# A transposed block by VectorE, both 32-blocks of a head in one product, and the decays of four heads in one product

## The chip, the cores and the metric

The kernel runs on one core of one Trainium2 chip. The metric is the device time of one execution in microseconds. The core has a matrix engine (TensorE, in the profile PE, its weight loads PEld), a vector engine (DVE), a scalar engine (ACT), GpSimd (POOL), and SyncE (SP), which issues most DMAs. Each engine works through a queue of its own in order, and semaphores tie the queues together.

## The reference

An encoder trunk with one hybrid layer (DEPTH is 1) over 2064 positions (16 meta tokens and 2048 inputs) with 1024 channels: layer norm, a combined input projection, a Fourier mixer and a gated DeltaNet side by side, gates, an output projection, and an MLP. The change touches the DeltaNet alone, which has 4 heads of 128 channels and runs in both directions. Cut to what matters:

```python
def chunked_gated_delta_rule(q, k, v, beta, g):
    g_cum = jnp.cumsum(g, axis=-1)
    diff = g_cum[..., :, None] - g_cum[..., None, :]
    decay_incl = jnp.exp(jnp.where(lower_incl, diff, -jnp.inf))
    decay_strict = jnp.where(lower_strict, decay_incl, 0.0)
    l_mat = jnp.einsum("rbhncd,rbhnsd->rbhncs", k_beta, k) * decay_strict
    unit_lower = l_mat + jnp.eye(CHUNK, dtype=l_mat.dtype)
    rhs = jnp.concatenate([v_beta, k_beta * jnp.exp(g_cum)[..., None]], axis=-1)
    sol = lax.linalg.triangular_solve(unit_lower, rhs, left_side=True, lower=True, unit_diagonal=True)
    ...
    def step(S, inp):
        val, kcd, qd, at, kt, cd = inp
        v_new = val - jnp.einsum("rbhcd,rbhde->rbhce", kcd, S)
        o = jnp.einsum("rbhcd,rbhde->rbhce", qd, S) + jnp.einsum("rbhcs,rbhse->rbhce", at, v_new)
        S = S * cd[..., None, None] + jnp.einsum("rbhcd,rbhce->rbhde", kt, v_new)
        return S, o
```

So for each chunk, head and direction a matrix of decays is needed, and the inverse of a unit triangular matrix; the chunks are then scanned one after the other.

## The kernel before

The kernel uses chunks of 128 positions: 16 chunks, and a short one of 16 positions for the meta tokens. Matrix products of the projections and of the MLP take f16 operands in three partial products (`mm3`, L95 to L97) and are arranged as Strassen products. The DeltaNet's own products are in f32; the trace shows each of them as two instructions on TensorE.

The work around the change lies in two stages.

**The preparation** (from about 520 to 840 us). `phase_zg` runs the projections of the gates on TensorE, group after group, and calls `next(side)` between them; `side` is the generator `Delta.prep`. It calls `stage2` for every chunk. `stage2` first calls `decay` for each direction, 32 times in all, and once more for the meta chunk (`meta`).

- `decay` forms, for one chunk and direction, E = exp(sums of g between two positions) for four heads at once. For each head it multiplies a 0/1 triangle by the head's column of g on VectorE (L1064, tile `gT`). On TensorE a product of a bf16 identity with a table of 0 and -1e30 (L1067) starts the PSUM bank `psg`, and four products, one for each head, with `gT` as weights and another triangle as the moving operand, add the sums of g (L1070). ScalarE takes exp (L1073).
- Then `stage2` forms the products of keys and queries (L1092), scales them with E on VectorE (L1097 for N, L1100 for A), takes the 32x32 diagonal blocks out (`diag`), and writes N and A to DRAM.
- `invert_blocks` inverts the diagonal blocks on VectorE (L997, L999).
- At the end of `prep`, `solve` runs for step 0 in both directions, with its PSUM from the pool `psg`.

PSUM tiles `psg` come from a pool of 3.

**The scan** (`phase_delta`, 995 to 1243 us). For step s it runs `step(s, d)` for both directions d, and between their parts `solve(s + 1, d)`, with its PSUM tiles from the pool `psh`. The function `go` and the list of its calls write out by hand in which order the parts follow. The instructions of a queue are then ordered when the program is built, and the trace shows small departures from the source order.

- `step` has five f32 products of 128x128 per head: with the state (L1264 and L1272), with the inverse (L1281), into the state (L1289) and into the output (L1301). Between them stand VectorE (L1266, L1295, L1307 or L1309) and ScalarE (L1275, L1284).
- `solve` builds the inverse X of the 128x128 triangular matrix, and its transpose XT, from the four inverted 32x32 diagonal blocks (L1171 and L1172 put them in place). In a first round it joins each pair of 32-blocks to a 64-block, in a second round the two 64-blocks. The first round is: product N by XT for each of the two pairs of a head (L1178), minus the result to V on ScalarE (L1181), product V by X (L1185), a further product X by V that gives one off-diagonal block transposed (L1187), a copy of that one to XT on ScalarE (L1188), and copies to X on VectorE (L1190). The second round is L1194, L1195, L1199 and L1200.

In `solve`, `blk(b)` is the b-th range of 32, `pair(a, z)` the z-th block of pair a, and f, s are 0, 1 in the forward direction and 1, 0 in the backward one. `cols(t, h, z)` takes, for head h, the z-th 32 columns of both pairs, 64 columns in all.

Of the kernel before, what the change touches and what calls it, by code (L numbers as in the profile page):

```python
# [12 lines left out]
AF = mybir.ActivationFunctionType  # L13
ALU = mybir.AluOpType
# [12 lines left out]
HD = 4  # L27
# [980 lines left out]
class Delta:  # L1008
# [48 lines left out]
    def decay(self, n, d, r):  # L1057

        k, nc, sp = self.k, self.k.nc, self.sp
        gs = k.g[:r, n, 4 * d:4 * d + 4]  # L1060
        gT = sp.tile([P, HD, P], F32, name="gT", bufs=2)
        m = (k.tls, k.tus)[d][:r, :r]
        for h in range(HD):
            nc.vector.tensor_scalar(gT[:r, h, :r], m, gs[:, h:h + 1], None, op0=ALU.mult)  # L1064
        yield
        ps = self.pg.tile([P, HD, P], F32, name="psg")
        nc.tensor.matmul(ps[:r, :, :r], lhsT=self.idb[:r, :r],  # L1067
                         rhs=self.mneg[:r, d, :r].unsqueeze(1).broadcast_to([r, HD, r]), start=True, stop=False)
        for h in range(HD):
            nc.tensor.matmul(ps[:r, h, :r], lhsT=gT[:r, h, :r], rhs=(k.tui, k.tli)[d][:r, :r],  # L1070
                             start=False, stop=h == HD - 1)
        E = sp.tile([P, HD, P], F32, name="E", bufs=2)
        nc.scalar.activation(out=E[:r, :, :r], in_=ps[:r, :, :r], func=AF.Exp)  # L1073
        return E
# [82 lines left out]
    def solve(self, step, d, sp, pp, pname):  # L1157

        k, nc = self.k, self.k.nc
        N = self.N[step, d]  # L1160
        ad = sp.tile([P, HD, 32], F32, name="ad", bufs=2)
        o = ((step % 4) * 2 + d) * 16
        (nc.scalar if step == 1 else nc.sync).dma_start(out=ad, in_=self.d2[step // 4][o:o + 16].rearrange("(h b) r j -> (b r) h j", b=4))
        X, XT, V, W = self.X[d][step % 2], self.XT[d], self.V[d], self.W[d]
        blk = lambda b: slice(32 * b, 32 * b + 32)
        half = lambda a: slice(64 * a, 64 * a + 64)
        f, s = ((0, 1), (1, 0))[d]
        pair = lambda a, z: blk(2 * a + z)
        x, xt = (XT, X) if d == 0 else (X, XT)
        for b in range(4):  # L1170
            nc.vector.transpose(xt[blk(b), :, blk(b)], ad[blk(b)])  # L1171
            nc.scalar.copy(x[blk(b), :, blk(b)], ad[blk(b)])  # L1172
        yield
        cols = lambda t, h, z: t[:, h].rearrange("p (a z c) -> p a z c", z=2, c=32)[:, :, z]
        ps = pp.tile([P, HD, P], F32, name=pname)
        for h in range(HD):
            for a in range(2):
                nc.tensor.matmul(ps[:32, h, blk(a)], lhsT=N[:, h, pair(a, s)], rhs=XT[:, h, pair(a, f)],  # L1178
                                 start=True, stop=True)
        for a in range(2):  # L1180
            nc.scalar.activation(out=V[pair(a, s), :, blk(a)], in_=ps[:32, :, blk(a)], func=AF.Copy, scale=-1.0)  # L1181
        yield
        ps = pp.tile([P, HD, P], F32, name=pname)
        for h in range(HD):
            nc.tensor.matmul(ps[:64, h, :64], lhsT=V[:, h], rhs=cols(X, h, s), start=True, stop=True)  # L1185
        for h in range(HD):
            nc.tensor.matmul(ps[:32, h, 64:96], lhsT=X[:, h, pair(f, s)], rhs=V[:, h, blk(f)], start=True, stop=True)  # L1187
        nc.scalar.copy(XT[pair(f, s), :, pair(f, f)], ps[:32, :, 64:96])  # L1188
        for a in range(2):
            nc.vector.tensor_copy(X[pair(a, f), :, pair(a, s)], ps[blk(a), :, blk(a)])  # L1190
        yield
        ps = pp.tile([P, HD, P], F32, name=pname)
        for h in range(HD):
            nc.tensor.matmul(ps[:64, h, :64], lhsT=N[:, h, half(s)], rhs=XT[:, h, half(f)], start=True, stop=True)  # L1194
        nc.scalar.activation(out=W[half(s)], in_=ps[:64, :, :64], func=AF.Copy, scale=-1.0)  # L1195
        yield
        ps = pp.tile([P, HD, P], F32, name=pname)
        for h in range(HD):
            nc.tensor.matmul(ps[:64, h, :64], lhsT=W[:, h], rhs=X[:, h, half(s)], start=True, stop=True)  # L1199
        nc.vector.tensor_copy(X[half(f), :, half(s)], ps[:64, :, :64])  # L1200
# [734 lines left out]
```

## Time and profile before

| | |
|---|---|
| median of 3 runs | 2729.1 us (2728.21 to 2729.52) |
| the profiled execution | 2723.02 us |
| span of its profile | 2721.2 us |
| mean granted TensorE clock | 0.988 |
| solves (32), products of L1178 | 8 each, 16 instructions |
| decays | 32 of 128 positions, one of 16 |

The profile is of one execution. A row of a timeline has the start in us, the length in us, the engine, the line of the kernel, the operation, output and inputs, the shapes, and how many instructions follow each other; in square brackets stands the idle time before it and what ended that. `128*32 128x32` means that 128 rows by 32 columns of weights are in the array, and 128x32 is the moving operand. Lengths of instructions that follow each other overlap, on TensorE above all: what one costs is read from start to start. A row of a group has the count, then the busy time in us, the mean length of one in ns, and the idle time of the engine just before them with what ended most of it. A row of waits has the engine and line that waited, what it waited for, the total in us, how often, and the longest.

### The profile page before, as it was taken

How to read it: one execution, taken by the hardware profiler on the slowest of the kernel's cores; microseconds unless marked ns; L12 is line 12 of the kernel's file. 1: busy time of each engine (PE TensorE's matmuls, PEld its weight loads, DVE VectorE, ACT ScalarE, POOL GpSimd, SP SyncE). 2: the span in 40 equal slices, each digit the busy share in tenths (PEclk: the TensorE clock that was granted, in tenths of full speed). 3: DMA queues.
4: the chain of work that ended last, by engine and by line, in shares of the span. 5: the costliest groups of instructions: out<-in, count | busy, mean ns of one | idle time of the engine just before them, and what ended most of it. 6: DMA issues, size and time to landing. Idle time of an engine off the chain costs nothing.

```text
span 2721.2 us, 42002 instructions
## 1 busy us (share of the span) xinstructions
PE 2604.6 (96%) x15087; PEld 1394.3 (51%) x15087; DVE 1950.3 (72%) x3793; ACT 1212.5 (45%) x2784; POOL 402.0 (15%) x559
## 2 busy tenths in 40 slices
PE   7988999999899989999999999999999999999997
PEld 6455545555454459995444444444444444444443
DVE  7589887888877326687867688888888645554556
ACT  5444665655553335674222544444454432222232
POOL 1000231310100001362256400000001200000003
PEclk9999999999999999999999999999999999999999
DMA  7468476699888758766722874444447633333311
GB/s 262 157 209 301 167 252 170 198 289 304 280 307 304 245 187 250 232 204 195 233 87 84 237 255 152 148 142 144 155 171 269 225 105 102 104 101 101 101 42 74
DMA packets 321219, 513.39 MB, mean 189 GB/s; under 512 B 83697, under 2 KB 135873, under 8 KB 317041
## 3 DMA queue, kind: packets, MB, share of 16 engines
q1 hardware_dynamic: 317088, 506.30, 56.5%
q10 hardware_dynamic: 3920, 4.40, 0.5%
q8 instruction: 118, 1.93, 0.3%
q14 instruction: 93, 0.75, 0.1%
HBM read 307.10 MB, written 203.50 MB: 188 GB/s over the span
## 4 chain that ended last, share of the span: by engine, by line
PE 67%; DVE 12%; DMA 6%; POOL 4%; ACT 3%; issue 3%; SPq 1%; DVEq 0%; POOLq 0%; ACTq 0%
PE mm L95 17%; PE mm L97 17%; PE mm L96 17%; DVE wu L59 1%; PE psc L1264 1%; PE psc L1289 1%; PE psc L1281 1%; PE psc L1301 1%; DVE hid L529 1%; PE psc L1272 1%; PE psf L95 1%; PE psm L95 1%; POOL hr L1412 1%; PE psm L97 1%; PE psm L96 1%
## 5 line engine op out<-in xcount | busy, mean ns | idle before, releaser
L95 PE MATMUL mm<-hb,wu 128*128 128x512 f16 x1280 | 487.1, 381 | 5.0 <-ACT ex L485 2.3
L97 PE MATMUL mm<-hb,wu 128*128 128x512 f16 x1280 | 487.3, 381 | 0.0
L96 PE MATMUL mm<-hb,wu 128*128 128x512 f16 x1280 | 487.2, 381 | 0.0
L1626 DVE TENSOR_TENSOR acc<-acc,mm 128x512 f32<-128x512 f32 x420 | 285.7, 684 | 147.9 <-PE mm L97 147.2
L95 PE MATMUL mm<-wdn,hid 128*128 128x512 f16 x904 | 342.1, 379 | 13.4 <-DVE acc L1626 13.3
L96 PE MATMUL mm<-wdn,hid 128*128 128x512 f16 x904 | 342.4, 379 | 0.0
L97 PE MATMUL mm<-wdn,hid 128*128 128x512 f16 x904 | 342.2, 379 | 0.2 <-DVE hid L529 0.2
L96 PEld LDWEIGHTS <-wu 128*128 128x128 f16 x1912 | 185.8, 98 | 218.7 <-issue 16.9
L97 PEld LDWEIGHTS <-wu 128*128 128x128 f16 x1912 | 185.6, 98 | 216.9 <-issue 7.4
L95 PEld LDWEIGHTS <-wu 128*128 128x128 f16 x1912 | 186.0, 98 | 210.3 <-issue 5.1
L95 PE MATMUL mm<-ht,wu 128*128 128x512 f16 x512 | 194.6, 380 | 5.5 <-DVE c L652 3.4
L529 DVE TENSOR_TENSOR hid<-c,hid 128x512 f16<-128x512 f32 x158 | 107.7, 688 | 124.8 <-ACT hid L528 124.6
L96 PE MATMUL mm<-ht,wu 128*128 128x512 f16 x512 | 194.5, 380 | 0.0
L97 PE MATMUL mm<-ht,wu 128*128 128x512 f16 x512 | 194.3, 380 | 0.0
L66 POOL TENSOR_SCALAR ln_rs<-ln_mv 128x1 f32<-128x1 f32 (+1 forms) x49 | 14.0, 285 | 1171.0 <-DVE ln_mv L76 1160.9
L528 ACT CAST hid<-c 128x512 f16<-128x512 f32 x158 | 95.7, 614 | 183.8 <-PE mm L97 155.2
L96 PEld LDWEIGHTS <-hid 128*128 128x128 f16 x904 | 88.4, 98 | 122.7 <-issue 19.8
L800 DVE SCALAR_TENSOR_TENSOR conv<-rawc,cw,conv 128x512 f32<-128x512 f32 x192 | 134.8, 744 | 15.4 <-ACT conv L798 14.9
L58 ACT ACTIVATE wdn<-raw 128x512 f16<-128x512 f32 x78 | 46.4, 622 | 222.7 <-PE mm L97 187.3
L97 PEld LDWEIGHTS <-hid 128*128 128x128 f16 x904 | 88.3, 98 | 108.1 <-DVE hid L529 2.2
L95 PEld LDWEIGHTS <-hid 128*128 128x128 f16 x904 | 88.4, 98 | 107.2 <-ACT hid L528 1.2
L58 ACT ACTIVATE wu<-raw 128x512 f16<-128x512 f32 x145 | 88.0, 622 | 74.4 <-PE mm L97 37.2
(388 smaller groups left out, 4999.5 us busy)
## 6 DMA issues: line engine op xcount, KB each, us to landing
wu<-op SPq DMA_DIRECT2D x245, 256.0 KB
op<-wu SPq DMA_DIRECT2D x203, 256.0 KB
wdn<-op SPq DMA_DIRECT2D x112, 256.0 KB
op<-wdn SPq DMA_DIRECT2D x98, 256.0 KB
kq<-kqd SPq DMA_DIRECT2D x46, 512.0 KB
raw<-in_w_down SPq DMA_DIRECT2D x36, 512.0 KB
raw<-in_w_qz SPq DMA_DIRECT2D x32, 512.0 KB
gt<-c SPq DMA_DIRECT2D x64, 256.0 KB
```

The costliest lines, as they stand in the source:

```text
L58: nc.scalar.activation(out=hi, in_=src, func=AF.Copy, scale=scale)
L59: nc.vector.scalar_tensor_tensor(out=lo, in0=src, scalar=scale, in1=hi, op0=ALU.mult, op1=ALU.subtract)
L95: mm(ps, lhsT=whi(q), rhs=xhi(q), start=first and q == 0, stop=False, skip_group_check=skip)
L96: mm(ps, lhsT=whi(q), rhs=xlo(q), start=False, stop=False, skip_group_check=skip)
L97: mm(ps, lhsT=wlo(q), rhs=xhi(q), start=False, stop=last and q == nk - 1, skip_group_check=skip)
L528: k.nc.scalar.copy(t[:, 0], src)
L529: k.nc.vector.tensor_tensor(out=t[:, 1], in0=src, in1=t[:, 0], op=ALU.subtract)
L800: nc.vector.scalar_tensor_tensor(out=s, in0=src[:, j:j + m], scalar=cw[:, c, j:j + 1], in1=s, op0=ALU.mult, op1=ALU.add)
L1264: nc.tensor.matmul(ps[:, h], lhsT=kq[:, h, 0], rhs=S[:, h], start=True, stop=True)
L1272: nc.tensor.matmul(psq[:, h], lhsT=kq[:, h, 1], rhs=S[:, h], start=True, stop=True)
L1281: nc.tensor.matmul(psv[:, h], lhsT=T_[:, h], rhs=R[:, h], start=True, stop=True)
L1626: nc.vector.tensor_tensor(out=c, in0=c, in1=ps, op=ALU.add)
```

## The change

In `decay` the four TENSOR_SCALAR of VectorE become one TENSOR_TENSOR over four heads, with both operands broadcast: the triangle over the heads, g over the columns. The two triangles trade places, so that the weights are the same for all heads and `gT` is the moving operand; the four products become one with 512 moving columns. The sums are the same ones.

In `solve` the two products of a head at L1178 become one: its weights are all 128 columns of N, its moving operand the 64 columns of XT that both products used. The two wanted 32x32 blocks then lie at other partitions of the PSUM tile, and L1181 reads them there. The product at L1187 is left out. The block that it gave is taken from the result of L1185, by a transpose of 32x32 blocks on VectorE, ahead of the two copies at L1190; ScalarE's copy (L1188) goes.

```diff
         gT = sp.tile([P, HD, P], F32, name="gT", bufs=2)
-        m = (k.tls, k.tus)[d][:r, :r]
-        for h in range(HD):
-            nc.vector.tensor_scalar(gT[:r, h, :r], m, gs[:, h:h + 1], None, op0=ALU.mult)
+        m = (k.tui, k.tli)[d][:r, :r]
+        nc.vector.tensor_tensor(out=gT[:r, :, :r], in0=m.unsqueeze(1).broadcast_to([r, HD, r]),
+                                in1=gs.unsqueeze(2).broadcast_to([r, HD, r]), op=ALU.mult)
         yield
...
-        for h in range(HD):
-            nc.tensor.matmul(ps[:r, h, :r], lhsT=gT[:r, h, :r], rhs=(k.tui, k.tli)[d][:r, :r],
-                             start=False, stop=h == HD - 1)
+        nc.tensor.matmul(ps[:r, :, :r], lhsT=(k.tls, k.tus)[d][:r, :r], rhs=gT[:r, :, :r], start=False, stop=True)
...
         for h in range(HD):
-            for a in range(2):
-                nc.tensor.matmul(ps[:32, h, blk(a)], lhsT=N[:, h, pair(a, s)], rhs=XT[:, h, pair(a, f)],
-                                 start=True, stop=True)
+            nc.tensor.matmul(ps[:, h, :64], lhsT=N[:, h], rhs=cols(XT, h, f), start=True, stop=True)
         for a in range(2):
-            nc.scalar.activation(out=V[pair(a, s), :, blk(a)], in_=ps[:32, :, blk(a)], func=AF.Copy, scale=-1.0)
+            nc.scalar.activation(out=V[pair(a, s), :, blk(a)], in_=ps[pair(a, s), :, blk(a)], func=AF.Copy, scale=-1.0)
         yield
...
-        for h in range(HD):
-            nc.tensor.matmul(ps[:32, h, 64:96], lhsT=X[:, h, pair(f, s)], rhs=V[:, h, blk(f)], start=True, stop=True)
-        nc.scalar.copy(XT[pair(f, s), :, pair(f, f)], ps[:32, :, 64:96])
+        nc.vector.transpose(XT[pair(f, s), :, pair(f, f)], ps[blk(f), :, blk(f)])
         for a in range(2):
             nc.vector.tensor_copy(X[pair(a, f), :, pair(a, s)], ps[blk(a), :, blk(a)])
```

## The prediction

> **What bounds the kernel now.** I read the page first, then the busy times by stage, then TensorE's order of instructions inside one step.
>
> ```profile
> span 2721.2 us, 42002 instructions
> PE 2604.6 (96%) x15087; PEld 1394.3 (51%) x15087; DVE 1950.3 (72%) x3793; ACT 1212.5 (45%) x2784; POOL 402.0 (15%) x559
> ...
> 520.00:775.00 255.00, 239.94 (x1235) 137.19 (x1234) 215.86 (x647) 142.95 (x305) 39.14 (x129) 0.99 0.88 286
> ...
> 1154.30:1170.90 16.60, 16.55 (x186) 15.08 (x186) 16.30 (x38) 13.58 (x54) 10.98 (x15) 1.00 0.80 252
> 1170.90:1187.50 16.60, 16.60 (x187) 15.16 (x186) 15.98 (x39) 13.34 (x53) 11.24 (x16) 1.00 0.80 236
> 995.00:1243.00 248.00, 245.89 (x2712) 225.09 (x2713) 176.48 (x509) 165.67 (x624) 89.27 (x114) 0.99 0.71 217
> ```
>
> The stage rows give the window, its length, then busy time of PE, PEld, DVE, ACT and POOL, the granted clock, the DMA share and GB/s. Two stages hold the edits. In 520 to 775 the decays are made beside the gate projections: PE is idle for 255.00 - 239.94 = 15.1 us, DVE for 39. In 995 to 1243 the 16 steps of the scan run: PE is idle for 2.1 us of 248. So in the scan every microsecond taken from PE comes off the end; in the preparation only what shortens PE's work or one of its 15 us of waits does.
>
> **The block inverse on TensorE.** One step, TensorE's row of the timeline (start, length, line, count):
>
> ```profile
> 1060.90 1.06 PE L1272 MATMUL psc<-S,kq 128*128 128x128 f32 x8
> 1061.79 1.06 PE L1281 MATMUL psc<-vt,hb 128*128 128x128 f32 x8
> 1062.78 0.69 PE L1178 MATMUL psh<-hb,N 128*32 128x32 f32 x16
> 1063.40 1.16 PE L1289 MATMUL psc<-vn,ktk 128*128 128x128 f32 x8
> 1064.49 0.68 PE L1185 MATMUL psh<-hb 128*64 128x64 f32 x8
> 1065.10 0.44 PE L1187 MATMUL psh<-hb 128*32 128x32 f32 x8
> 1065.46 1.16 PE L1289 MATMUL psc<-vn,ktk 128*128 128x128 f32 x8
> ...
> 1067.45 0.68 PE L1185 MATMUL psh<-hb 128*64 128x64 f32 x8
> ...
> 1068.42 1.16 PE L1301 MATMUL psc<-vn,A 128*128 128x128 f32 x8
> 1069.51 1.15 PE L1194 MATMUL psh<-hb,N 128*64 128x64 f32 x16
> 1070.72 0.68 PE L1199 MATMUL psh<-hb 128*64 128x64 f32 x8
> 1071.32 0.49 PE L1264 MATMUL psc<-S,kq 128*128 128x128 f32 x2
> 1071.76 0.68 PE L1199 MATMUL psh<-hb 128*64 128x64 f32 x8
> ...
> L1178 PE MATMUL psh<-hb,N x480: 196/196/263, 995.3 to 1225.3; 128*32 128x32 f32 x160
> ```
>
> An f32 product is two instructions, so x16 at L1178 is the eight products of one solve, and 480 / 16 = 30 solves lie in this stage (the other two are in the preparation). Eight 128-column pairs in a row cost 1061.79 - 1060.90 = 0.89 us, 0.111 each. L1281 would thus be done at 1061.79 + 0.89 = 1062.68 if another 128-column block followed. L1289 starts at 1063.40, and its length is 1.16 instead of 1.06, so it really begins 0.10 later, at 1063.50: **L1178 costs 0.82 us**. Its 16 pairs alone run at (0.69 - 0.20) / 16 = 0.031 each, 0.49; the other 0.33 goes where the block's width changes from 128 to 32 columns and back. L1187 costs 1065.46 - 1065.10 = **0.36 us** (eight pairs at 0.031 and one more change of width).
>
> After the change L1178 is four products, eight pairs, with 128 columns of weights and 64 moving columns, and no change of width on either side. L1187 is gone, and L1185 changes width straight back to 128. What a pair of 128 and 64 costs no row shows. If the weight load sets it, 0.111 as between L1272 and L1281; if the moving columns do, (1.15 - 0.22) / 16 = 0.058 as in L1194.
>
> ```profile
> L1281 PEld LDWEIGHTS psc<-vt,hb 128*128 128x128 f32 x96 | 11.6, 191 | 0.2
> L1185 PEld LDWEIGHTS psh<-hb 128*64 128x64 f32 x96 | 6.5, 137 | 1.4
> L1187 PEld LDWEIGHTS psh<-hb 128*32 128x32 f32 x96 | 3.9, 112 | 0.8
> ```
>
> A load's mean grows by (191 - 137) / 64 = 0.84 ns per column. The part that cannot overlap the next load is thus about 128 x 0.84 = 108 ns, nearly the whole 111 of a pair: I take 0.111, that is 8 x 0.111 = 0.89 for the block, **+0.07**. The bounds are 8 x 0.058 = 0.46 (-0.36) and, with each load standing in line for its full 191 ns, 1.53 (+0.71). The Trainium skill says the same of the load, and it speaks against this edit: by "TensorE: Matmul & The Clock Gate", section "LDWEIGHTS (loading the stationary operand)", a load takes its columns divided by 1.2 ns, whatever the depth. By that rule the block would be at least 8 x 107 ns = 0.85 us, so merging the two 32-column products saves nothing by itself; the three load rows agree with its slope. The skill also has a rule for the other side: "TensorEngine Tiling (Array Packing)", section "Key Properties", says that changing the tiling mode drains TensorE. The 0.33 us at L1178 agrees; were there no such drain, the old block would be 0.49 and the edit +0.40.
>
> Per solve: +0.07 - 0.36 = -0.29. For the scan: 30 x -0.29 = **-8.7 us**. The two solves in the preparation give **-0.6**.
>
> **The transposed block on DVE.** ACT loses the copy at L1188, DVE gains a transpose of a 32x128 block out of PSUM.
>
> ```profile
> L1171 DVE STREAM_TRANSPOSE hb<-ad 32x128 f32<-32x128 f32 x52 | 15.6, 301 | 13.7 <-PE psh L1178 5.2 <-PE psc L1281 5.1 <-DMA ad<-d 1.6
> L1190 DVE COPY hb<-psh 32x128 f32<-32x128 f32 x24 | 6.8, 283 | 5.8 <-ACT hb L1188 5.5
> ...
> 1067.89 0.68 DVE L1307 TENSOR_TENSOR o<-psc,qs 128x512 f32<-128x512 f32 x1
> 1068.59 0.25 ACT L1188 COPY hb<-psh 32x128 f32<-32x128 f32 x1 [2.06 <-PE psh L1187]
> 1068.87 0.58 DVE L1190 COPY hb<-psh 32x128 f32<-32x128 f32 x2 [0.29 <-ACT hb L1188]
> ```
>
> The SBUF transpose of this size is 0.30, a PSUM copy of it 0.28; I take 0.30, at most 0.42 if the PSUM source costs as much again as a half. L1190 waits for L1188 today, so the transpose stands in a place where DVE was waiting for ACT anyway. In the step above: L1185 of the second direction ends near 1068.05, DVE is in L1307 until 1068.57, the transpose would be done at 1068.9. The first reader is the second half of L1194, behind eight pairs of L1301 and eight of L1194, near 1069.7 on the shortened queue: 0.8 us of cover. What pays is DVE's load: 2 x 0.30 per step. Over the stage DVE has 248 - 176 = 72 us free, but in the two windows quoted (1154 to 1187) it is busy for 16.30 and 15.98 of 16.60. There DVE would need 16.9 and 16.6 while PE would need 16.0, so these two steps keep their length: **+1.2 us** given back.
>
> In the preparation there is one more place:
>
> ```profile
> PE psg L1194 <- ACT hb L1188: 3.4, 1, 3.4
> ...
> 831.35 0.63 ACT L58 ACTIVATE hb<-raw 128x512 f16<-128x512 f32 x1 [0.51 <-DMA op<-hb]
> 832.01 0.25 ACT L1188 COPY hb<-psg 32x128 f32<-32x128 f32 x1
> 832.90 0.28 DVE L1190 COPY hb<-psg 32x128 f32<-32x128 f32 x1
> ```
>
> TensorE stands for 3.4 us because L1188 is queued on ACT behind casts that wait for DMA. That copy goes; the transpose will stand in DVE's queue, where L1190 ran at 832.90, among other work. Between nothing and -3.4 I take half: **-1.7**.
>
> **The decays.** Per decay four products of 128 moving columns become one of 512, and four TENSOR_SCALAR become one TENSOR_TENSOR.
>
> ```profile
> L1064 DVE TENSOR_SCALAR gT<-cst,g 128x128 f32<-128x128 f32 x128 | 28.7, 287 | 0.1
> L819 DVE TENSOR_TENSOR vt<-pst,sqk 128x512 f32<-128x512 f32 x3 | 2.1, 690 | 1.7 <-PE pst L815 1.1 <-issue 0.6
> ...
> 749.21 1.73 PE psg L1092 x8
> ...
> 765.46 0.89 PE psg L1070 x8
> ...
> PE psg L1067 <- DVE A L1100: 1.7, 1, 1.7
> PE psg L1067 <- DVE A L1100: 5.2, 2, 3.5
> PE psg L1070 <- DVE gT L1064: 0.9, 1, 0.9
> ```
>
> L1070 costs eight pairs, 0.89 us, now. L1092 is the f32 product with 256 moving columns: 1.73 / 8 = 0.216 per pair, twice 0.111 less a little, so the price goes with the moving columns. Two pairs of 512 are 2 x 0.43 = 0.86: -0.03 each, 32 times, **-1.0 us**. The merged product saves TensorE almost nothing. DVE goes from 4 x 0.287 = 1.15 to 0.69 (the broadcast product at L819 shows it, 0.80 at most), -0.46 x 32 = 15 us of DVE work. TensorE waits for DVE there in the three places quoted: 1.7 (before 640), 5.2 (after) and 0.9, 7.8 us in all; the first two kinds end when L1100 has read an older result and frees its PSUM buffer. Two sets of decays lie in the queue ahead of such a wait, so about 0.9 us less of each of the three longest: **-3**, between 0 and -7.8. With it the wait passes to others that are named in the same view, ACT's E (L1073) among them.
>
> **Sum.** -8.7 - 0.6 + 1.2 - 1.7 - 1.0 - 3.0 = -13.8. The profiled execution took 2723.02 us (span 2721.2, 1.8 around it) and would take 2709.2; the median of the runs is 2729.1, 6.1 above, and with the same difference I forecast 2729.1 - 13.8 = **2715.3 us**, 0.5% less.
>
> **The rivals.**
> The moving columns set the new pair, not the load. Then L1178 costs 0.46 instead of 0.89, 32 x -0.43 = -13.8 more: 2701.5. For it: every pair in the trace has as many moving columns as weight columns or more, so no row separates the two. Against: the slope of the load rows, which alone gives 108 ns. Chance 0.12.
>
> DVE gets late. The transpose is queued behind work that waits for a later product: were it behind the second L1307, which waits for L1301 ending at 1069.5, it would finish near 1070.5, 0.8 after its reader is due. On the second direction of 15 steps, about 0.6 each, that is +9: 2724.3. Queue order here is not source order (L1264 of the next step runs between the two L1199 of this one, last rows of the step's timeline), so it can happen; against it, L1190 stands ahead of the second L1307 today. It decides from 0.8 us of delay. Chance 0.14.
>
> Loads do not overlap short products. With the full 191 ns per pair the block costs 1.53, +0.64 over my value, 32 x 0.64 = +20.5: 2735.8, slower by 0.25%. The place is L1178 alone, and it decides when a pair takes more than 0.147 us, (0.82 + 0.36) / 8, where the scan stops gaining. Against it: 32-column loads of 112 ns follow each other every 31 ns. Chance 0.05.
>
> The preparation returns nothing, or loses some us to another order of its queues (DVE's order interleaves the decays with other work): the scan's -7.5 is left and up to 4 goes back, 2718 to 2726. Chance 0.14; the forecast itself has 0.55.
>
> **How the numbers follow.** The forecast's own bounds: without both halved waits and the decays 2721, with all of them 2709. The range takes in the first rival below and the late DVE above: 2700 to 2725. What lies under 2723.6 (faster by over 0.2%, about what a measurement of this kernel tells from no change) is the forecast 0.55, the first rival 0.12 and some two thirds of the last: 0.77. Within 0.2%: most of the late DVE and the rest, 0.16. Slower: 0.07.
>
> **What would show it.** L1178 as x8 with starts 0.111 apart, and 0.89 between its neighbours; the L1289 behind it at 1.06, not 1.16; no L1187, and 0.61 from L1185 to the next 128-column block; steps of 15.1 us instead of 15.7; the transpose near 0.30, ending before L1194; in the preparation L1070 as x2 at 0.43 and shorter waits of L1067. Pairs at 0.058, or waits of L1194 or L1199 for DVE, would make the prediction wrong.

## The result and the profile after

The changed kernel takes 2716.17 us (median of 4 runs, 2714.17 to 2719.81) against 2729.31 us; the ratio is 0.9949 with a 95% interval of 0.9935 to 0.9964. Timed again beside its parts it gave 0.9947 (0.9933 to 0.9960): 14.5 us less, between 10.9 and 18.3. The forecast was 13.8 us less, 2715.3 us.

The profiled execution of the changed kernel took 2715.62 us (span 2713.8), only 7.4 us less than that of the kernel before. That is a matter of which execution was profiled: the kernel before ran between 2721.5 and 2733.8 us in 25 runs, and the 2723.02 us of its profile lie near the lower end. So the sizes below are taken from the ratios and from steps that repeat in every execution, not from the difference of two spans.

Busy time in the scan of the changed kernel (window, its length, then PE, PEld, DVE, ACT, POOL, granted clock, DMA share, GB/s):

```profile
992.50:1232.60 240.10, 237.67 (x2234) 223.16 (x2235) 182.45 (x536) 158.78 (x594) 92.05 (x114) 0.99 0.72 220
```

The scan runs for 240.1 us instead of 248, and TensorE is still idle for 2.4 us only: it was the bound and is the bound. VectorE is busy for 6 us more there. In the profile of the second timing the scan of the changed kernel lasts 242.1 us (998.78 to 1240.89); the step that repeats is the same, and it is the start of the scan that is longer.

One step of the scan, TensorE's timeline of the changed kernel (L1175 is the old L1178, L1181 the old L1185, L1275 the old L1281, L1283 the old L1289, L1266 the old L1272):

```profile
1056.42 1.06 PE L1266 MATMUL psc<-S,kq 128*128 128x128 f32 x8
1057.31 1.06 PE L1275 MATMUL psc<-vt,hb 128*128 128x128 f32 x8
1058.20 1.00 PE L1175 MATMUL psh<-hb,N 128*128 128x64 f32 x8
1059.04 1.11 PE L1283 MATMUL psc<-vn,ktk 128*128 128x128 f32 x8
1060.08 0.68 PE L1181 MATMUL psh<-hb 128*64 128x64 f32 x8
1060.69 1.16 PE L1283 MATMUL psc<-vn,ktk 128*128 128x128 f32 x8
...
1067.12 0.68 PE L1193 MATMUL psh<-hb 128*64 128x64 f32 x8 [0.35 <-ACT hb L1189]
...
1088.77 1.00 PE L1175 MATMUL psh<-hb,N 128*128 128x64 f32 x8
...
1103.91 1.00 PE L1175 MATMUL psh<-hb,N 128*128 128x64 f32 x8
```

L1175 starts 0.89 behind L1275, so no time goes for a change of width. From L1175 to L1283 it is 0.84, and L1283's row is 0.05 longer than one behind an equal block (1.11 against the 1.06 that the prediction named), read as a beginning that much later: the block costs 0.89 us. L1187 is gone; from L1181 to the next block it is 0.61. The last two rows are the same block in two steps, 15.14 us apart; the step before and the step after them last 15.13 and 15.14. The first step shown is 15.44, because L1193 (the old L1199) waits in it for ScalarE. The kernel before has 1078.52 - 1062.78 = 15.74, the first row of this pair being in the prediction:

```profile
1078.52 0.69 PE L1178 MATMUL psh<-hb,N 128*32 128x32 f32 x16
```

TensorE's waits in the preparation of the changed kernel (what waited, for what, total us, times, longest), beside the ones quoted in the prediction:

```profile
PE psg L1188 <- DVE hb L1182: 3.3, 1, 3.3
PE psg L1067 <- DVE A L1098: 3.2, 4, 1.3
...
PE psg L1069 <- DVE gT L1063: 0.2, 1, 0.2
```

L1067 waits for VectorE for 3.2 us instead of 6.9, and the product of the decays for `gT` for 0.2 instead of 0.9. The wait of the second solve (L1188, the old L1194) is 3.3, where it was 3.4, with VectorE's transpose at its end instead of ScalarE's copy.

### The profile page after: what moved, and what is told of

Read it like the earlier page. It is cut to its first block, busy times and chain, and to the rows that moved or that the text cites. A ratio compares the mean times of both kernels' runs of the same rounds, so it can differ in the third digit from the quotient of the medians.

```text
span 2713.8 us, 40453 instructions
## 1 busy us (share of the span) xinstructions
PE 2596.9 (96%) x14377; PEld 1371.4 (51%) x14377; DVE 1953.1 (72%) x3726; ACT 1206.4 (44%) x2752; POOL 402.3 (15%) x559
## 4 chain that ended last, share of the span: by engine, by line
PE 62%; DVE 16%; DMA 7%; ACT 4%; issue 4%; POOL 3%; SPq 1%; DVEq 0%; POOLq 0%; ACTq 0%
PE mm L95 17%; PE mm L97 16%; PE mm L96 16%; DVE wu L59 2%; DVE hb L59 1%; DVE hid L529 1%; PE psc L1258 1%; DVE conv L800 1%; DVE acc L1620 1%; PE psc L1295 1%; PE psc L1283 1%; PE psh L1175 1%; PE psc L1266 1%; POOL hr L1406 1%; PE psc L1275 1%
```

## The experiments

Theory A is the prediction's: TensorE bounds the scan; there the wide product costs 0.07 us a solve, the dropped product gives 0.36, and the decays help only through VectorE in the preparation. Its rivals are named with each run. All ratios are to the kernel before, with 95% intervals.

**The whole change again.**

> The changed kernel as it is, timed again beside its parts. Theory A (the scan is bound by TensorE, each solve costs it 0.29 us less; the preparation gives the rest): 0.9949 again, 12 to 15 us less than before. Theory B (the two profiled executions tell the whole difference, 2723.0 and 2715.6): about 7 us less, 0.9973.

Measured: 0.9947 (0.9933 to 0.9960), 2713.68 us. The interval leaves out 0.9973, the ratio of the two profiled executions. Theory B falls.

**The decays alone.**

```diff
-            nc.tensor.matmul(ps[:r, h, :r], lhsT=gT[:r, h, :r], rhs=(k.tui, k.tli)[d][:r, :r],
-                             start=False, stop=h == HD - 1)
+        nc.tensor.matmul(ps[:r, :, :r], lhsT=(k.tls, k.tus)[d][:r, :r], rhs=gT[:r, :, :r], start=False, stop=True)
```

(with the one TENSOR_TENSOR for `gT`; `solve` as in the kernel before)

> Only the decays are changed. Theory A: TensorE's products gain 1 us, shorter waits for VectorE in the preparation 3 us: 3 to 5 us less than before, the scan (first L1178 to the first f16 product after it) stays at 248.2 us. Rival (VectorE's 15 us of saved work is what pays): 8 to 15 us less, and the solve alone gives nearly nothing.

Measured: 0.9988 (0.9977 to 0.9999), that is 3.3 us less, between 0.3 and 6.3. From its timeline, the narrow product of the second direction in two steps, and from its waits in the preparation:

```profile
1084.03 0.69 PE L1176 MATMUL psh<-hb,N 128*32 128x32 f32 x16
...
1099.77 0.69 PE L1176 MATMUL psh<-hb,N 128*32 128x32 f32 x16
...
PE psg L1067 <- DVE A L1098: 2.0, 3, 0.8
```

The step stays at 15.74, and the waits for VectorE shrink. Both fit theory A. The scan as a whole missed its expectation: it lasts 250.0 us (983.94 to 1233.98) instead of 248.2. The excess lies in its first step and in one later step, and the kernel before, profiled again, has 248.7. That VectorE's saved 15 us pay as such is out, since the interval ends at 6.3.

**The block inverse alone**, both of its edits, the decays as before.

```diff
-            for a in range(2):
-                nc.tensor.matmul(ps[:32, h, blk(a)], lhsT=N[:, h, pair(a, s)], rhs=XT[:, h, pair(a, f)],
+            nc.tensor.matmul(ps[:, h, :64], lhsT=N[:, h], rhs=cols(XT, h, f), start=True, stop=True)
...
-        nc.scalar.copy(XT[pair(f, s), :, pair(f, f)], ps[:32, :, 64:96])
+        nc.vector.transpose(XT[pair(f, s), :, pair(f, f)], ps[blk(f), :, blk(f)])
```

> Only the block inverse is changed, both of its edits. Theory A: the scan gets 8 us shorter (248.2 to about 240), the time by 7 to 10 us; in the preparation the wait of about 3.4 us before the second solve's third product stays, since the transpose on VectorE is as late as ScalarE's copy was. Rival (decays pay): 0 to 3 us less.

Measured: 0.9968 (0.9957 to 0.9979), 8.7 us less, between 5.7 and 11.7. The wide block of the second direction in two steps of the timeline, and the wait in the preparation:

```profile
1093.27 1.00 PE L1177 MATMUL psh<-hb,N 128*128 128x64 f32 x8
...
1108.40 1.00 PE L1177 MATMUL psh<-hb,N 128*128 128x64 f32 x8
...
PE psg L1190 <- DVE hb L1184: 3.4, 1, 3.4
```

15.13 us a step, and the wait is there in full. The scan lasts 241.4 us (994.96 to 1236.40), 6.8 less than in the first profile of the kernel before and 7.3 less than in the second, where 8 was expected. The two parts add up to 12.0 of the 14.5 us, inside the intervals.

**The kernel before, profiled again.** Not a line is changed.

> The kernel before, for a second profile of it. If the stages behind the scan (from 1243 us to the end, 1478 us) differ by 1 to 4 us from the first profile, then the 3.4 us that they are longer by in the changed kernel's profile are no effect of the change. If they agree within 0.3 us, the change has made them longer.

Measured: 0.9993 (0.9982 to 1.0004) against itself. Its scan repeats: the block of the second direction at

```profile
1093.10 0.69 PE L1178 MATMUL psh<-hb,N 128*32 128x32 f32 x16
...
1108.83 0.69 PE L1178 MATMUL psh<-hb,N 128*32 128x32 f32 x16
```

15.73 us apart. The last f32 products of the scan, in this profile, in the first one and in the changed kernel's (count, lengths, then the first and the last start):

```profile
L1328 PE MATMUL psc<-ident,qs x64: 272/273/331, 1146.9 to 1251.1; 128*128 128x128 f32 x64
L1328 PE MATMUL psc<-ident,qs x64: 272/273/331, 1148.0 to 1252.0; 128*128 128x128 f32 x64
L1322 PE MATMUL psc<-ident,qs x64: 272/273/329, 1140.3 to 1241.2; 128*128 128x128 f32 x64
```

The last one starts at 1251.1 and the span ends at 2724.3, 1473.2 us later; in the first profile it is 2721.2 - 1252.0 = 1469.2, and in the changed kernel's 2713.8 - 1241.2 = 1472.6. The stages behind the scan vary by 4.0 us between two executions of one kernel; the 3.4 us that they were longer by in the changed kernel's profile are within that. The stages ahead of the scan vary as well: it starts at 995.3 and 993.9 in the two profiles of the kernel before, and at 992.5 and 998.8 in the two of the changed kernel.

**The wide product alone**, with the product at L1187 and its copy kept, and the decays as before.

```diff
-            for a in range(2):
-                nc.tensor.matmul(ps[:32, h, blk(a)], lhsT=N[:, h, pair(a, s)], rhs=XT[:, h, pair(a, f)],
-                                 start=True, stop=True)
+            nc.tensor.matmul(ps[:, h, :64], lhsT=N[:, h], rhs=cols(XT, h, f), start=True, stop=True)
         for a in range(2):
-            nc.scalar.activation(out=V[pair(a, s), :, blk(a)], in_=ps[:32, :, blk(a)], func=AF.Copy, scale=-1.0)
+            nc.scalar.activation(out=V[pair(a, s), :, blk(a)], in_=ps[pair(a, s), :, blk(a)], func=AF.Copy, scale=-1.0)
```

> From the kernel before, only the first product of the block inverse is made wide (four products with 128 columns of weights and 64 moving ones in place of eight of 32 by 32); the product that gives the transposed block and its copy stay, the decays too. Theory A (the load of 128 columns sets the pair at 0.111 us; two changes of width are saved): the block costs 0.89 instead of 0.82, 30 x 0.07 = 2 us more than before in the scan, the time unchanged within 0.1% or 2 us up. Rival 1 (the moving columns set it, 0.058): 11 us less. Rival 2 (the width changes cost nothing by themselves): 0.40 a solve, 12 us more.

Measured: 0.9999 (0.9989 to 1.0009). In its timeline the same block in two steps:

```profile
1052.43 1.11 PE L1287 MATMUL psc<-vn,ktk 128*128 128x128 f32 x8
...
1068.32 1.11 PE L1287 MATMUL psc<-vn,ktk 128*128 128x128 f32 x8
```

15.89 us, 0.15 more than the 15.74 of before, 0.075 a solve where 0.07 was forecast. Putting both blocks of a head into one product, by itself, costs a little. Both rivals (11 us less, 12 us more) are out.

**The transposed block alone**, with the eight narrow products and the decays as before.

```diff
-        for h in range(HD):
-            nc.tensor.matmul(ps[:32, h, 64:96], lhsT=X[:, h, pair(f, s)], rhs=V[:, h, blk(f)], start=True, stop=True)
-        nc.scalar.copy(XT[pair(f, s), :, pair(f, f)], ps[:32, :, 64:96])
+        nc.vector.transpose(XT[pair(f, s), :, pair(f, f)], ps[blk(f), :, blk(f)])
```

> From the kernel before, only the transposed block is taken by VectorE: the product and ScalarE's copy go, the eight narrow products and the decays stay. Theory A: 0.36 us of TensorE less per solve, 30 x 0.36 = 11 us less in the scan, 10 to 12 us less in all. Rival (the transpose makes VectorE late, and the next product waits): under 5 us less, with waits of the third product for the transpose.

Measured: 0.9966 (0.9953 to 0.9979), 9.3 us less, between 5.7 and 12.8, where 10 to 12 were expected. Two steps of its timeline, and one block of a late step:

```profile
1091.98 0.69 PE L1178 MATMUL psh<-hb,N 128*32 128x32 f32 x16
...
1106.96 0.69 PE L1178 MATMUL psh<-hb,N 128*32 128x32 f32 x16
...
1169.71 0.25 PE L1178 MATMUL psh<-hb,N 128*32 128x32 f32 x2
1169.89 0.49 PE L1287 MATMUL psc<-vn,ktk 128*128 128x128 f32 x2
1170.31 0.63 PE L1178 MATMUL psh<-hb,N 128*32 128x32 f32 x14
```

14.98 us, 0.76 less, 0.38 a solve. The waits that the rival asked for are not in the scan. The late steps gain less, 0.95 us in three of them (1148.06 to 1196.97, against 3 x 16.62 before): there L1178 of the second direction is cut in two by another product, as in the last rows, so that TensorE visits the 32-column weights once more. So in the steps that repeat the whole gain of the block inverse comes from the product that is left out, and the wide product takes 0.15 of it back in each step.

**All 128 moving columns**, from the changed kernel; the further columns of the result are not read.

```diff
-            nc.tensor.matmul(ps[:, h, :64], lhsT=N[:, h], rhs=cols(XT, h, f), start=True, stop=True)
+            nc.tensor.matmul(ps[:, h], lhsT=N[:, h], rhs=XT[:, h], start=True, stop=True)
...
-            nc.scalar.activation(out=V[pair(a, s), :, blk(a)], in_=ps[pair(a, s), :, blk(a)], func=AF.Copy, scale=-1.0)
+            nc.scalar.activation(out=V[pair(a, s), :, blk(a)], in_=ps[pair(a, s), :, pair(a, f)], func=AF.Copy, scale=-1.0)
```

> From the changed kernel, the wide product's moving operand is all 128 columns of XT instead of the 64 that are used; the further columns of the result are not read. Theory A (the load sets the pair): starts stay 0.111 apart, the block stays at 0.89 us and the scan within 1 us of the changed kernel's 240 to 242. Rival (moving columns): the pair goes from 0.058 to 0.111.

Measured: one run of 2720.75 us. In its timeline and its waits in the scan:

```profile
1052.52 1.06 PE L1175 MATMUL psh<-hb,N 128*128 128x128 f32 x8
1053.42 1.06 PE L1275 MATMUL psc<-vt,hb 128*128 128x128 f32 x8
...
1067.66 1.06 PE L1175 MATMUL psh<-hb,N 128*128 128x128 f32 x8
...
PE psh L1193 <- ACT hb L1189: 5.5, 2, 4.7
```

The block takes 0.90 us and the step 15.14, as with 64 moving columns: twice the moving columns cost nothing, so the load sets the pair. That rests on the steps that repeat in one execution. The scan as a whole missed its expectation, 242.5 us to the first f16 product but with f32 products left behind it, above all because of the one wait of 4.7 us: L1189 stood on ScalarE behind a cast that waited for a DMA of `w_delta`. I take that for an accident of queues and DMA and not for the price of the columns; no run tests it.

**96 columns of weights**, from the changed kernel.

```diff
-            nc.tensor.matmul(ps[:, h, :64], lhsT=N[:, h], rhs=cols(XT, h, f), start=True, stop=True)
+            nc.tensor.matmul(ps[:96, h, :64], lhsT=N[:, h, 32 * s:32 * s + 96], rhs=cols(XT, h, f), start=True, stop=True)
...
-            nc.scalar.activation(out=V[pair(a, s), :, blk(a)], in_=ps[pair(a, s), :, blk(a)], func=AF.Copy, scale=-1.0)
+            nc.scalar.activation(out=V[pair(a, s), :, blk(a)], in_=ps[blk(2 * a), :, blk(a)], func=AF.Copy, scale=-1.0)
```

> From the changed kernel, the wide product loads 96 columns of N (from the first wanted block to the end of the second) instead of 128. Theory A (the load's columns set the pair, 0.84 ns each, and 96 columns need no change of width beside 128): 0.084 a pair, 0.22 us less per solve, 6 to 7 us less than the changed kernel (0.9947 goes to about 0.992). Rival (the array is set up for 128 columns whatever is loaded, or 96 counts as another width): no gain or a loss of up to 0.3 a solve, 9 us.

Measured: 0.9934 (0.9921 to 0.9946), 2710.02 us. Its timeline, and the group of its loads beside that of the changed kernel (count, busy us, mean ns):

```profile
1059.40 0.81 PE L1175 MATMUL psh<-hb,N 128*96 128x64 f32 x8
1060.05 1.11 PE L1275 MATMUL psc<-vt,hb 128*128 128x128 f32 x8
...
1092.30 0.81 PE L1175 MATMUL psh<-hb,N 128*96 128x64 f32 x8
...
1107.06 0.81 PE L1175 MATMUL psh<-hb,N 128*96 128x64 f32 x8
...
L1175 PEld LDWEIGHTS psh<-hb,N 128*96 128x96 f32 x104 | 10.2, 165 | 0.0
```

```profile
L1175 PEld LDWEIGHTS psh<-hb,N 128*128 128x128 f32 x106 | 13.0, 192 | 0.0
```

From L1175 to L1275 it is 0.65 instead of 0.84, the block 0.70, 0.088 a pair. The step is 14.76, 0.38 less than the changed kernel's 15.14, or 5.7 us in 15 steps; 6 to 7 were expected. The load's mean falls by (192 - 165) / 32 = 0.84 ns a column, the slope on which the prediction took its value. The two ratios are 3.5 us apart and their intervals overlap; the step shows the gain, the total alone would not.

**The second products side by side**, from the changed kernel: only the order of the calls.

```diff
-            go(st[0])
-            go(ho[0])
-            go(st[1])
-            go(st[0])
-            go(ho[1])
-            go(st[1])
+            go(st[0], st[0])
+            go(ho[0], ho[1])
+            go(st[1], st[1])
```

> From the changed kernel, only the order of the scan's parts is changed: the two directions' second products of the block inverse (L1181) follow each other, after both of the first direction's last products. Theory A (each visit to 64-column weights costs 0.35 us of TensorE beside the pairs): one visit less per step, 15 x 0.35 = 5 us less than the changed kernel. Rival (a chain through ScalarE or VectorE ends up later than what it covers now): the visit's gain comes back as waits of L1188 or L1283, same time or more.

Measured: 0.9930 (0.9917 to 0.9944), 2710.49 us. Its timeline:

```profile
1053.62 1.00 PE L1175 MATMUL psh<-hb,N 128*128 128x64 f32 x8
...
1059.96 1.15 PE L1181 MATMUL psh<-hb 128*64 128x64 f32 x16
1061.04 1.16 PE L1283 MATMUL psc<-vn,ktk 128*128 128x128 f32 x8
...
1068.43 1.00 PE L1175 MATMUL psh<-hb,N 128*128 128x64 f32 x8
...
1079.88 0.68 PE L1193 MATMUL psh<-hb 128*64 128x64 f32 x8 [0.90 <-ACT hb L1189]
```

L1181 now runs as x16, and the step is 14.81, 0.33 less: one change to 64 columns and back, 0.35 by theory A. The next step lasts 15.66 us: L1193 waits in it for ScalarE for 0.90. So some of the gain does come back as a wait, though of another product than the rival named, and in one of the steps that repeat. The scan lasts 235.9 us (992.99 to 1228.85), against 240.1 and 242.1 in the changed kernel.

**Both of the last two edits.**

```diff
+            nc.tensor.matmul(ps[:96, h, :64], lhsT=N[:, h, 32 * s:32 * s + 96], rhs=cols(XT, h, f), start=True, stop=True)
...
+            go(st[0], st[0])
+            go(ho[0], ho[1])
+            go(st[1], st[1])
```

> Both of the last two edits on the changed kernel: 96 columns of weights and the new order. Theory A: the two gains add, 6 to 7 and 5 us, 2702 to 2706 us, a ratio to the kernel before near 0.991. Rival (shorter covers make new waits): no better than the better one of the two alone.

Measured: 0.9920 (0.9906 to 0.9935), 2706.34 us, the fastest of all.

```profile
1052.72 0.81 PE L1175 MATMUL psh<-hb,N 128*96 128x64 f32 x8
...
1067.16 0.81 PE L1175 MATMUL psh<-hb,N 128*96 128x64 f32 x8
```

14.44 us a step: 0.70 less than the changed kernel, where 0.38 and 0.33 add up to 0.71. The two gains add in this step. The one after it lasts 14.93, with a wait of L1193 for ScalarE as in the last run. The total lies just above the 2702 to 2706 that were expected, and its interval overlaps those of the two edits alone, so it is the step and the scan that speak against the rival: the scan lasts 232.3 us, against 237.3 and 235.9 with one of the edits.

## Why the prediction was right, point by point

**TensorE bounds the scan.** Shown: the step that repeats follows the sum of its blocks on TensorE, 15.74, 15.89, 14.98 and 15.14 us for before, the wide product, the transpose and both.

**The wide product, +0.07 a solve.** Shown twice: the block is 0.89 us, set by the load (128 moving columns cost the same), and alone it makes the step 0.15 longer. The rival by which the moving columns set the pair is out, and so is the one by which short products leave the whole load uncovered.

**The dropped product, -0.36 a solve.** Measured 0.38. With the wide product 15.74 - 15.14 = 0.60 a step, 0.30 a solve; forecast 0.29.

**VectorE full in two late steps, +1.2.** The reason was wrong. Other late steps of the kernel before last as long with VectorE far from full, and what each has on TensorE beyond an early step is L1328, twice four instructions (the last two rows are busy times by window):

```profile
1165.27 0.60 PE L1328 MATMUL psc<-ident,qs 128*128 128x128 f32 x4
...
1166.88 0.66 PE L1328 MATMUL psc<-ident,qs 128*128 128x128 f32 x4
...
1187.50:1204.10 16.60, 16.60 (x186) 15.16 (x185) 13.32 (x36) 12.72 (x50) 10.16 (x15) 1.00 0.70 208
...
1220.40:1237.00 16.60, 16.60 (x186) 15.16 (x185) 11.30 (x31) 10.45 (x42) 9.29 (x15) 1.00 0.21 59
```

VectorE is busy there for 13.32 and 11.30 of 16.60 us. Eight pairs at 0.111 are 0.89, and 15.74 + 0.89 = 16.63 is the late step: TensorE sets it, as it sets the early ones. Five late steps together, before and in the changed kernel (from one L1272, now L1266, to the fifth after it):

```profile
1154.13:1236.89 82.76, 82.71 (x922) 75.67 (x921) 69.90 (x177) 62.70 (x249) 50.52 (x70) 1.00 0.60 180
```

```profile
1145.48:1226.04 80.56, 79.78 (x762) 74.73 (x761) 74.06 (x199) 62.26 (x240) 52.09 (x70) 1.00 0.65 194
```

They gain 2.20 us, where five times 0.60 is 3.00. TensorE's busy time falls by 2.93, and it is idle for 0.78 us where it was idle for 0.05; the waits that the trace lists in these steps are for a product of TensorE itself (0.4) and for ScalarE (0.2), none for VectorE. In two other profiles with the same block inverse the five steps last 80.24 (the whole change again) and 79.85 (the block inverse alone). So 0.1 to 0.8 us go back, not 1.2, and little of it in the two steps named: those got shorter by 0.57 and 0.43, from 16.63 and 16.62 to 16.06 and 16.19. The step that failed is to take a measured busy time of 16.30 as work that has to fit into that one step. The casts of `wd` (L59) fall unevenly on the steps: the first of the two held three of them, the changed kernel's hold one and two.

**The second solve's wait, -1.7.** Wrong: 3.3 us where it was 3.4, and 3.4 in the block inverse alone. The transpose stands in VectorE's queue at 825.20, behind casts, adds and the inverse of the diagonal blocks (L997), the first of which waited for a DMA until 820.08. ScalarE's copy stood in the same way behind casts that waited for a DMA:

```profile
820.08 0.20 DVE L997 TENSOR_TENSOR ivt<-ivq 128x30 f32<-128x30 f32 x1 [4.58 <-DMA ivq<-d]
...
824.87 0.31 DVE L997 TENSOR_TENSOR ivt<-ivq 128x150 f32<-128x150 f32 x1
...
825.20 0.31 DVE L1182 STREAM_TRANSPOSE hb<-psg 32x128 f32<-32x128 f32 x1
...
825.57 0.68 PE L1188 MATMUL psg<-hb 128*64 128x64 f32 x8 [3.34 <-DVE hb L1182]
```

The work moved to another engine, and the wait moved with it. By the prediction's own words a wait of L1194 for VectorE would make it wrong; in the scan of the changed kernel there is none, here there is this one. Half of the wait was a middle between two ends, not a reading.

**The decays, -1.0 on TensorE and -3 in waits.** The product is x2 and takes 0.86 us, VectorE's product 0.68 where 0.69 was forecast. L1067's wait for VectorE is 5.4 to 6.9 us in the five profiles with the old decays, and 2.0 to 3.3 in six of the seven with the new ones (5.2 in that of the 96 columns); the means, 6.1 and 3.2, are 2.9 apart. The decays alone gave 3.3 us (0.3 to 6.3) against 4.0 forecast, which the interval cannot tell apart. How much of a wait saved there passes to another one was not measured: the stages ahead of the scan vary by up to 6.3 us between two executions of one kernel (992.5 and 998.8).

**The sum.** 13.8 forecast, 14.5 measured (10.9 to 18.3). The block inverse alone was -8.7 - 0.6 + 1.2 - 1.7 = -9.8 and gave 8.7 (5.7 to 11.7). The two small terms that were off have opposite signs: 1.7 us did not come, and 0.4 to 1.1 less than forecast was given back in the late steps. That they cancel in part is luck, and the total would have hidden them. The -0.6 of the two solves in the preparation was not measured by itself.

## What to carry to other kernels

In this scan, where TensorE is the bound, merging f32 products of few columns into one with wide weights is priced by the columns loaded, not by the number of instructions: it cost 0.15 us a step, while a product left out and a visit to another weight width avoided gave 0.76 and 0.33. Load only the columns that span what is wanted, and put products of equal weight width next to each other. A wait in front of a queue was not removed by moving its last link to another engine whose queue is held up in the same way. And a busy engine is not yet the one that sets the time: look for steps of the same length in which it is less busy.

## What was not expected of the hardware

96 columns of weights beside blocks of 128 cost no change of width: behind the 96-column block L1275 has 1.11 as its length, as behind the 128-column block, where L1283 behind 64 columns has 1.16 and starts 0.61 behind a block whose eight pairs would take 0.46. And the 64 moving columns leave no trace in time: with the load at 0.112 a pair, products of 64 and of 128 moving columns give steps of the same 15.14 us.
